# Hybrid decoder trunk: a planner that makes two plans, one with stretched times, redraws parts of each, and picks one by trial executions

## The chip, the cores and the metric

The kernel runs on one core of a Trainium2 chip, in one launch. The metric is the device time of one execution in microseconds (us), over several executions; lower is better. All times here are of this one core. PE is TensorE's matmul path, PEld its weight loads, DVE is VectorE, ACT is ScalarE, POOL is GpSimd and SP is SyncE, which issues most of the transfers.

## The reference

Two layers of a decoder on 1024 tokens of width 1024, in float32. Cut to what matters:

```python
def reference(x, attn_norm, w_in, ..., w_o, ffn_norm, w_gate_up, w_down, final_norm):
    for l in range(DEPTH):                         # 2
        h = rmsnorm(x, attn_norm[l])
        proj = h @ w_in[l]
        (c_q, c_kv, k_r, g_b, g_c, u_conv, u_pool, q_sw, k_sw, v_sw) = jnp.split(proj, pts, axis=-1)
        y_a = mla_attention(...)                   # 4 heads, causal over all keys
        y_b = short_gated_conv(...)                # causal, width 3
        y_c = multiscale_pool(...)                 # causal means over 2, 4, 8, 16
        y_d = swa_sink_attention(...)              # 4 heads, window of 128
        groups = jnp.stack([y_a, y_b, y_c, y_d], axis=2)
        gf = groups * lax.rsqrt(jnp.mean(groups * groups, axis=-1, keepdims=True) + RMS_EPS)
        x = x + (gf.reshape(b, s, D_MIX) * mix_norm[l]) @ w_o[l]
        h2 = rmsnorm(x, ffn_norm[l])
        gate, up = jnp.split(h2 @ w_gate_up[l], 2, axis=-1)
        x = x + (jax.nn.silu(gate) * up) @ w_down[l]     # D_FF = 2816
    return rmsnorm(x, final_norm)
```

## The kernel before

**The work.** Activations lie transposed, 128 channels on the partitions by 512 tokens, so a tile is 128 x 512 and the tokens make two halves. Each float32 operand is split into two fp32r parts, a rounded one and the rest, and `mm3` (L316) makes each product with three matmuls of up to 512 columns (recorded at L322). `split` (L340) makes the two parts: ACT copies the rounded one (L342), DVE subtracts it (L345). This is done for weights as they arrive and for activations as they are made. The two FFN products are done by a scheme with seven in place of eight block products: POOL and DVE form sums and differences of blocks (weights in `GateUp.sums`, L1260 to L1262; activations in `combine`, L1179 to L1200, and in `combos`, L1511 to L1516, which also stores them to HBM as `ad`), and the down projection loads `ad` again. The gate's step for an FFN block begins in `gu_start`; its L1380 takes a product out of PSUM on DVE. L421 is the common elementwise product on DVE, L1228 adds the output projection to the residual, L1309 and L1318 take first FFN products out of PSUM, L1500 and L1502 are the SiLU on ACT and the multiplication after it on POOL.

**Buffers.** Nearly all tiles live in 47 slots of 128 x 1024 (`u0` to `u46`, class `Slots`), and products in eight PSUM banks. Which slot a tile takes is decided as the program is written out: in turn, or, where planned times are given (`ends`), the slot whose last tile is planned to end first. The banks likewise: by fixed turns, or as a list (`given`).

**The order.** The program is first written out straight, and then ordered by a planner, class `Order` (L1858). It reads the written instructions and their dependencies, gives each a time on its engine (`costs`, L1934; for a DVE `TensorTensor` of n columns 0.15 + n x 0.001045 us, for a load its bytes' time + 2.1 us), and `run` (L1984) executes them on five queues, PE, ACT, DVE, POOL and SP: whenever an engine is free it takes the instruction of lowest rank among those that are ready. A load is taken to land 1.5 us late (`LATE`). While a DVE instruction with two inputs in SBUF and a POOL sum overlap, the later one is made to wait. `find` (L2055) goes forward with the written order as rank, back from the end to get a rank by urgency, and forward again, three forward runs in all, and keeps the shortest. `banks` (L2070) and `ends` (L2082) draw banks and slots from the planned times; they need a new writing-out, and so a new plan. `scheduled_kernel` (L2102) does this round four times, keeps the round with the shortest plan, and imposes its order on each queue (`impose`, L2089: each instruction is put behind the one before it, without a semaphore).

So every engine works its queue off strictly in the planned order. If the first in a queue waits on the chip longer than was planned, all behind it wait too.

Of the kernel before, what the change touches and what calls it, by code (L numbers as in the profile page):

```python
# [35 lines left out]
HALVES = (1, 0)  # L36
OUT_PARTS = tuple((d, t) for d in range(NK) for t in HALVES)
N_U = 47

NSP = 3  # L40
NG = NFF // 2
# [12 lines left out]
class Slots:  # L54
# [3 lines left out]
    def __init__(self, pool, n, ends=None):  # L58
        self.pool = pool
        self.ends = iter(ends) if ends else None  # L60
        self.until = [0.0] * n
        self.asked = []
        self.places = deque(range(n))
        self.halves = {F32: deque(), F32R: deque()}
        self.cur = [None] * n
        self.dt = [None] * n
# [56 lines left out]
def trunk_kernel(ctx: ExitStack, tc: tile.TileContext, ins, out, given=None, ends=None):  # L123
# [9 lines left out]

    slots = Slots(ctx.enter_context(tc.tile_pool(name="slots", bufs=1)), N_U, ends)
    R, F = View(slots, F32R), View(slots, F32)
# [1722 lines left out]
class Order:  # L1858
# [7 lines left out]
    SHARED = 1.3  # L1866
    LEAST = 0.14

    def __init__(self, traced, edges, banks=True):
        self.n = len(traced)  # L1870
        self.engine = [self.queue(i) for i in traced]
        self.cost = [self.costs(i) for i in traced]
        self.kind = [self.kinds(i) for i in traced]
        self.moved = [self.passing(i) for i in traced]
        place = {i.name: k for k, i in enumerate(traced)}
        need = [{} for _ in traced]
        users = self.users = defaultdict(list)
        for k, i in enumerate(traced):
            for m in {a.memref for a in (*i.outs, *i.ins) if hasattr(a, "memref")}:
                users[m].append(k)  # L1880
        freed = [set() for _ in traced]
        for k, i in enumerate(traced):
            for name, kind in edges(i.name):
                if name in place:
                    p = place[name]
                    need[k][p] = need[k].get(p, False) or "NoSync" not in str(kind)
                elif banks or self.engine[k] != "PE":
                    freed[k].update(place[x] for x, _ in edges(name) if x in place)
            for p in freed[k]:
                need[k][p] = True  # L1890
        for m, ks in users.items():
            made = [freed[k] for k in ks if any(m == getattr(a, "memref", 0) for a in traced[k].outs)]
            for p in set().union(*made).difference(ks):
                for k in ks:
                    if p < ks[0]:
                        need[k][p] = True
        self.need = [list(d.items()) for d in need]
        self.feeds = [[] for _ in traced]
        for k, d in enumerate(self.need):
            for p, sync in d:  # L1900
                self.feeds[p].append((k, sync))
# [79 lines left out]
            return 0.29 + n * 0.00098, 0.21 + n * 0.00098  # L1981
        return t, t - 0.083

    def run(self, rank, back=False):  # L1984

        ahead, wait = (self.need, self.feeds) if back else (self.feeds, self.need)
        late, cost, kind = self.LATE[back], self.cost, self.kind  # L1990
        left = [len(w) for w in wait]
        ready, end, free = [0.0] * self.n, [0.0] * self.n, dict.fromkeys(self.ENGINES, 0.0)
        later = {e: [] for e in self.ENGINES}
        now = {e: [] for e in self.ENGINES}
        order = {e: [] for e in self.ENGINES}
        flying, served = deque(), 0.0
        port = {"two": 0.0, "pool": 0.0}
        other = {"two": "pool", "pool": "two"}
        for k in range(self.n):
            if not left[k]:  # L2000
                heapq.heappush(later[self.engine[k]], (0.0, k))

        def due(e, t):
            while later[e] and later[e][0][0] <= t:
                k = heapq.heappop(later[e])[1]
                heapq.heappush(now[e], (rank[k], k))

        for _ in range(self.n):
            best = None
            for e in self.ENGINES:  # L2010
                due(e, free[e])
                if not now[e] and not later[e]:
                    continue
                t = free[e] if now[e] else later[e][0][0]
                if e == "SP" and not back and len(flying) == self.LANES:
                    t = max(t, flying[0])
                if best is None or t < best[0]:
                    best = t, e
            t, e = best
            due(e, t)  # L2020
            k = heapq.heappop(now[e])[1]
            seen, taken = cost[k]
            order[e].append(k)
            if back:
                free[e] = t + taken * (self.SHARED if kind[k] == "pool" else 1.0)
                end[k] = -free[e]
            else:
                if kind[k] in port:
                    more = max(0.0, port[other[kind[k]]] - t - self.LEAST)
                    seen, taken = seen + more, taken + more  # L2030
                    port[kind[k]] = t + seen
                free[e], end[k] = t + taken, t + seen
                if self.moved[k]:
                    if kind[k] == "load":
                        end[k] += late
                    served = end[k] = max(end[k], served + self.moved[k])
                if e == "SP":
                    flying.append(end[k])
                    if len(flying) > self.LANES:
                        flying.popleft()  # L2040
            for j, sync in ahead[k]:
                if back:
                    s, o = cost[j]
                    if kind[j] == "load":
                        s += late
                    r = free[e] + (self.HOP[self.engine[j]] + s - o if sync else -o)
                else:
                    r = end[k] + self.HOP[e] if sync else t
                ready[j] = max(ready[j], r)
                left[j] -= 1  # L2050
                if not left[j]:
                    heapq.heappush(later[self.engine[j]], (ready[j], j))
        return end, order

    def find(self, passes=3):  # L2055
        rank, best = list(range(self.n)), None
        for _ in range(passes):
            end, order = self.run(rank)
            if best is None or max(end) < best[0]:
                best = max(end), order, end  # L2060
            rank, _ = self.run([-x for x in end], back=True)
        return best

    def tiles(self, prefix):


        found = (m for m in self.users if m.startswith(prefix) and m.rsplit("_", 1)[1].isdigit())
        return sorted(found, key=lambda m: int(m.rsplit("_", 1)[1]))
# [30 lines left out]
                )  # L2099


def scheduled_kernel(fresh, ins_of, rounds=4):  # L2102

    def trace(banks, ends, order=None):
        nc = fresh()
        ins, out = ins_of(nc)
        with tile.TileContext(nc) as tc:
            asked = trunk_kernel(tc, ins, out, banks, ends)  # L2110
            traced = [
                i
                for i in nc.cur_bb.bb.instructions
                if Order.queue(i) in Order.ENGINES and i.opcode != "TilePoolBoundary"
            ]
            if order is not None:
                Order.impose(tc, traced, order)
        return nc, traced, asked

    nc, traced, asked = trace(None, None)  # L2120
    plan = Order(traced, nc.dependency_edges)
    end, best = plan.find()[2], None
    for _ in range(rounds):
        given = plan.banks(end), plan.ends(end, asked)
        nc, traced, asked = trace(*given)
        plan = Order(traced, nc.dependency_edges)
        span, order, end = plan.find()
        if best is None or span < best[0]:
            best = span, given, order
    return trace(*best[1], best[2])[0]  # L2130


# [131 lines left out]
```

## Time and profile before

| | |
|---|---|
| time, median of 3 runs | 2047.57 us (2047.41 to 2049.72) |
| profiled execution | 2048.33 us, span 2046.5 us |
| PE busy | 2029.3 us, 9422 matmuls |
| DVE busy | 1518.8 us, 2443 instructions |
| ACT busy | 989.4 us, 1737 instructions |
| POOL busy | 541.2 us, 412 instructions |
| DMA over the span | 305.50 MB, 149 GB/s on the mean |

The profile is of one execution. The span goes from the first to the last instruction's end; the execution's own time has 1.8 us around it. Busy time is the union of an engine's instructions; the matmuls overlap in the pipeline, and their ends are modelled. The view of waits says for each engine how long it stood idle in front of which line, and which line's instruction ended that. The timeline gives start, length, engine, line, output and input, with the idle time before in brackets. In the windows view each row is a stretch of the span with the busy time and instruction count of each engine. The chain is followed back from the last instruction, at each step to what released it.

### The profile page before, as it was taken

The numbers are of one execution on the slowest core, as the hardware profiler recorded it, in microseconds if no ns is written. First come the engines' busy times: TensorE is split into PE (matmuls) and PEld (weight loads), VectorE is DVE, ScalarE is ACT, GpSimd is POOL, SyncE is SP. The second block draws the span as 40 slices with busy tenths as digits, with TensorE's granted clock in tenths as the row PEclk, the third lists the DMA queues.
The fourth block names the chain that finished last, engine by engine and source line by source line (L and its number), as shares of the span: only waits on it lengthen the run. The fifth ranks groups of instructions, "written<-read, shape, count | busy, mean of one in ns | idle before, by whom it ended". The sixth has DMA issues, their size and how long they took to land.

```text
span 2046.5 us, 26478 instructions
## 1 busy us (share of the span) xinstructions
PE 2029.3 (99%) x9422; PEld 1676.5 (82%) x9422; DVE 1518.8 (74%) x2443; ACT 989.4 (48%) x1737; POOL 541.2 (26%) x412
## 2 busy tenths in 40 slices
PE   9999999999999999999999999999999999999998
PEld 7887888878888888888888878888788888888887
DVE  8779978997666768546656898889966666676555
ACT  7447657753333335434533666667433333354342
POOL 0100000047786782010001000000577654410000
PEclk9999999999999999999999999999999999999999
DMA  5431232334645556997426413232455522287552
GB/s 207 104 66 42 77 102 84 136 134 157 204 168 190 180 172 253 287 279 223 157 71 139 107 52 110 70 114 106 150 190 169 184 106 93 86 289 265 179 187 86
DMA packets 141348, 305.50 MB, mean 149 GB/s; under 512 B 13728, under 2 KB 56736, under 8 KB 141216
## 3 DMA queue, kind: packets, MB, share of 16 engines
q1 hardware_dynamic: 130976, 280.74, 39.9%
q0 software_dynamic: 10240, 23.07, 5.8%
q8 instruction: 74, 1.21, 0.2%
q14 instruction: 58, 0.48, 0.1%
HBM read 225.11 MB, written 100.66 MB: 159 GB/s over the span
## 4 chain that ended last, share of the span: by engine, by line
PE 93%; DVE 3%; ACT 1%; issue 1%; DMA 1%; POOL 0%; DVEq 0%; ACTq 0%; POOLq 0%
PE ps_mm L322 36%; PE ps_s L322 29%; PE ps_t L322 11%; PE ps_pv L322 8%; PE ps_pv L1090 2%; PE ps_t L1078 1%; DVE u L345 1%; PE ps_s L1024 1%; PE ps_s L1026 1%; PE ps_s L1025 1%; DMA u<-in_w_gu 1%; PE ps_s L896 1%; PE ps_pv L699 1%; PE ps_s L638 1%; PE ps_t L405 1%
## 5 line engine op out<-in xcount | busy, mean ns | idle before, releaser
L322 PE MATMUL ps_mm<-u,u 128*128 128x512 f32 (+1 forms) x3378 | 831.0, 390 | 2.9 <-DVE tp L1380 1.3
L322 PEld LDWEIGHTS ps_mm<-u,u 128*128 128x128 f32 x3378 | 615.3, 188 | 128.7 <-issue 5.5
L322 PE MATMUL ps_s<-u,u 128*128 128x512 f32 x2670 | 634.4, 390 | 2.3 <-DVE u L345 1.7
L345 DVE TENSOR_TENSOR u<-u,u 128x1024 fp32r<-128x1024 f32 (+2 forms) x400 | 449.5, 1142 | 213.1 <-ACT u L342 154.8
L322 PEld LDWEIGHTS ps_s<-u,u 128*128 128x128 f32 x2670 | 500.4, 188 | 110.1 <-DVE u L345 4.0
L342 ACT CAST u<-u 128x1024 fp32r<-128x1024 f32 (+2 forms) x400 | 346.4, 882 | 452.8 <-DMA u<-ad 75.8
L322 PE MATMUL ps_t<-u,u 128*128 128x512 f32 (+1 forms) x1124 | 254.4, 378 | 0.4 <-DVE u L1309 0.4
L322 PEld LDWEIGHTS ps_t<-u,u 128*128 128x128 f32 x1124 | 202.0, 188 | 41.4 <-DVE u L1494 2.0
L1502 POOL TENSOR_TENSOR tp<-tp,u 128x512 f32<-128x512 f32 x80 | 129.6, 1620 | 362.2 <-ACT tp L1500 362.1
L322 PE MATMUL ps_pv<-u,u 128*128 128x512 f32 x744 | 177.1, 389 | 0.0
L322 PEld LDWEIGHTS ps_pv<-u,u 128*128 128x128 f32 x744 | 139.6, 188 | 29.1
L1500 ACT ACTIVATE tp<-tp 128x512 f32<-128x512 f32 x80 | 50.6, 632 | 151.2 <-DVE tp L421 151.1
L1087 POOL MEMSET u<- 128x128 f32 x32 | 6.1, 221 | 406.6 <-PE ps_pv L1090 134.1
L342 ACT CAST u<-ps_t 128x512 fp32r<-128x512 f32 (+3 forms) x132 | 65.0, 503 | 47.6 <-PE ps_t L1078 23.3
L345 DVE TENSOR_TENSOR u<-ps_t,u 128x512 fp32r<-128x512 f32 (+3 forms) x132 | 75.3, 581 | 11.7 <-ACT u L342 9.7
L348 DVE SCALAR_TENSOR_TENSOR u<-u,par,u 128x512 fp32r<-128x512 f32 x100 | 73.3, 745 | 13.1 <-ACT u L347 12.8
L347 ACT ACTIVATE u<-u,par 128x512 fp32r<-128x512 f32 x100 | 70.2, 716 | 26.6 <-DVE u L421 10.6
L386 ACT ACTIVATE tn<-u 128x512 f32<-128x512 f32 (+1 forms) x91 | 52.9, 596 | 55.5 <-DVE u L1771 46.8
L296 POOL DMA_DIRECT2D gd<-in_w_gu x24 | 21.3, 887 | 217.8 <-DMA gd<-in_w_gu 57.6
L1290 POOL TENSOR_TENSOR u<-u 128x512 f32<-128x512 f32 x38 | 67.5, 1776 | 40.0 <-DVE u L345 38.8
L421 DVE TENSOR_TENSOR tp<-tp,u 128x512 f32<-128x512 f32 x76 | 68.7, 904 | 1.7
L1580 POOL TENSOR_TENSOR u<-u,u 128x352 f32<-128x352 f32 x48 | 62.9, 1311 | 3.1 <-DMA u<-in_w_dn 2.0
(206 smaller groups left out, 2356.4 us busy)
## 6 DMA issues: line engine op xcount, KB each, us to landing
u<-in_w_gu SPq DMA_DIRECT2D x84, 512.0 KB, 4.1
ad<-u SPq DMA_DIRECT2D x154, 256.0 KB, 2.4
u<-ad SPq DMA_DIRECT2D x70, 512.0 KB, 5.5
u<-in_w_dn SPq DMA_DIRECT2D x48, 352.0 KB, 3.5
qd<-u SPq DMA_DIRECT2D x48, 352.0 KB, 2.6
u<-qd SPq DMA_DIRECT2D x32, 512.0 KB, 5.4
u<-in_w_in SPq DMA_DIRECT2D x28, 512.0 KB, 3.5
u<-in_w_dn SPq DMA_DIRECT2D x24, 512.0 KB, 5.4
```

Source lines behind the costliest of these rows:

```text
L322: last_mm = pe.matmul(o, w, r, start=start and k == 0 and i == 0, stop=stop and k == n - 1 and i == 2, skip_group_check=again,)
L342: a = act.copy(hi, f)
L345: dve.tensor_tensor(out=lo, in0=f, in1=rd(hi), op=ALU.subtract)
L347: a = act.activation(hi, f, AF.Copy, scale=gain)
L348: dve.scalar_tensor_tensor(out=lo, in0=f, scalar=gain, in1=rd(hi), op0=ALU.mult, op1=ALU.subtract)
L386: act.activation(q, f, AF.Square)
L421: dve.tensor_tensor(out=o, in0=a, in1=b, op=ALU.mult)
L1090: pe.matmul(py[:, c0:], v_of(j, h), R.ap(s)[:, c0:], start=j == 0 and n == 0, stop=j == nj - 1 and n == 1,)
L1290: pool.tensor_tensor(out=q4, in0=q4, in1=F.ap(self.raw[1] + 1), op=ALU.add)
L1500: last_silu = act.activation(g, g, AF.Silu)
L1502: pool.tensor_tensor(out=g, in0=g, in1=r, op=ALU.mult)
L1580: pool.tensor_tensor(out=o, in0=a, in1=b, op=ALU.add)
```

## The change

The instructions themselves stay as they are: no part of `trunk_kernel` is touched. What is new is how the planner finds the order, the slots and the banks.

- The rounds go from four to one, for each of two plans. The first plans with the times of `costs`, the second with the times of DVE and ACT instructions multiplied by 1.03 (`SLOW`). Each starts from the straight program's plan with the same factor.
- `improve` takes a plan and its rank and draws 30 times: it picks a planned wait of PE of over 0.05 us, with a chance by its length, adds Gaussian noise with a deviation of 1 us to the rank of every instruction that is planned to end between 40 us ahead of that wait and 5 us behind it, plans anew with it, and keeps the new rank where the plan is not longer.
- `trial` executes a finished order six times in the model, the queues in fixed order and with the unchanged times, where in each execution a DMA load is late with a chance of a quarter, by up to 2.5 us, and the times of DVE, ACT and POOL vary by 2%. The plan with the shorter mean is taken.

```diff
+SLOW = (1.0, 1.03)
...
-    def run(self, rank, back=False):
+    def run(self, rank, back=False, fixed=None, draw=None):
...
+        if fixed is None:
+            cost = [
+                (a * self.slow, b * self.slow) if e in ("DVE", "Activation") else (a, b)
+                for (a, b), e in zip(cost, self.engine)
+            ]
...
+                if fixed is not None:
+                    i = len(order[e])
+                    if i == len(fixed[e]) or left[fixed[e][i]]:
+                        continue
+                    t = max(free[e], ready[fixed[e][i]])
...
+            if draw:
+                late = 2.5 * draw.random() if draw.random() < 0.25 else 0.0
+                if e in ("DVE", "Activation", "Pool"):
+                    more = draw.gauss(0.0, 0.02) * seen
+                    seen, taken = seen + more, taken + more
...
+    def trial(self, order):
+        ends = (self.run(None, fixed=order, draw=random.Random(n))[0] for n in range(6))
+        return sum(map(max, ends)) / 6
...
+    def waits(self, order, end):
+        found, free = [], 0.0
+        for k in order["PE"]:
+            seen, taken = self.cost[k]
+            start = end[k] - seen
+            if start - free > 0.05:
+                found.append((start, start - free))
+            free = start + taken
+        return found
+
+    def improve(self, best, tries):
+        draw = random.Random(1)
+        span, order, end = best
+        rank, _ = self.run([-x for x in end], back=True)
+        e, o = self.run(rank)
+        if max(e) <= span:
+            span, order, end = max(e), o, e
+        found = self.waits(order, end)
+        for _ in range(tries):
+            at = draw.choices([t for t, _ in found], [w for _, w in found])[0]
+            new = [
+                r + draw.gauss(0.0, 1) if at - 40 < t < at + 5 else r for r, t in zip(rank, end)
+            ]
+            e, o = self.run(new)
+            if max(e) <= span:
+                rank, span, order, end = new, max(e), o, e
+                found = self.waits(order, end)
+        return span, order, end
...
-def scheduled_kernel(fresh, ins_of, rounds=4):
+def scheduled_kernel(fresh, ins_of, rounds=1):
...
-    plan = Order(traced, nc.dependency_edges)
-    end, best = plan.find()[2], None
-    for _ in range(rounds):
-        given = plan.banks(end), plan.ends(end, asked)
-        nc, traced, asked = trace(*given)
-        plan = Order(traced, nc.dependency_edges)
-        span, order, end = plan.find()
-        if best is None or span < best[0]:
-            best = span, given, order
+    first, tried, found = Order(traced, nc.dependency_edges), asked, []
+    for slow in SLOW:
+        plan, asked, first.slow = first, tried, slow
+        end = plan.find()[2]
+        for _ in range(rounds):
+            given = plan.banks(end), plan.ends(end, asked)
+            nc, traced, asked = trace(*given)
+            plan = Order(traced, nc.dependency_edges, slow)
+            best = plan.find()
+            end = best[2]
+            order = plan.improve(best, 30)[1]
+            found.append((plan.trial(order), given, order))
+    best = min(found, key=lambda x: x[0])
     return trace(*best[1], best[2])[0]
```

More of the change, by code (lines that the diff above doesn't have):

```diff
@@ L2 @@
 import math
+import random
 from collections import defaultdict, deque
@@ L1867, with __init__ @@
     LEAST = 0.14
-    def __init__(self, traced, edges, banks=True):
+    def __init__(self, traced, edges, slow=1.0, banks=True):
+        self.slow = slow
         self.n = len(traced)
@@ L2010, in run @@
             for e in self.ENGINES:
[L2011 to L2014, printed above, removed]
+                if fixed is not None:
[3 more added lines that the diff above has]
+                    t = max(free[e], ready[fixed[e][i]])
+                else:
+                    due(e, free[e])
+                    if not now[e] and not later[e]:
+                        continue
+                    t = free[e] if now[e] else later[e][0][0]
                 if e == "SP" and not back and len(flying) == self.LANES:
@@ L2019, in run @@
             t, e = best
-            due(e, t)
-            k = heapq.heappop(now[e])[1]
-            seen, taken = cost[k]
+            if fixed is not None:
+                k = fixed[e][len(order[e])]
+            else:
+                due(e, t)
+                k = heapq.heappop(now[e])[1]
+            seen, taken = cost[k]
+            if draw:
[3 more added lines that the diff above has]
+                    seen, taken = seen + more, taken + more
             order[e].append(k)
@@ L2050, in run @@
                 left[j] -= 1
-                if not left[j]:
+                if not left[j] and fixed is None:
                     heapq.heappush(later[self.engine[j]], (ready[j], j))
         return end, order
+    def trial(self, order):
+        ends = (self.run(None, fixed=order, draw=random.Random(n))[0] for n in range(6))
+        return sum(map(max, ends)) / 6
     def find(self, passes=3):
```

## The prediction

> **What bounds the kernel now.** I read the page first, its busy shares and its chain of what ended last.
>
> ```profile
> span 2046.5 us, 26478 instructions
> PE 2029.3 (99%) x9422; PEld 1676.5 (82%) x9422; DVE 1518.8 (74%) x2443; ACT 989.4 (48%) x1737; POOL 541.2 (26%) x412
> ...
> PE 93%; DVE 3%; ACT 1%; issue 1%; DMA 1%; POOL 0%; DVEq 0%; ACTq 0%; POOLq 0%
> ```
>
> TensorE (PE) is busy for 2029.3 of 2046.5 us and carries 93% of the chain; DVE, the next engine, is at 74%. So the work of PE sets the time, and the change can only move the 17.2 us in which PE is idle. How fast PE goes while it is busy comes from the groups by form and from the chain in order of time.
>
> ```profile
> L322 PE MATMUL ps_s<-u,u 128*128 128x512 f32 x2670 | 634.4, 390 | 2.3 <-DVE u L345 1.7 <-DVE u L1228 0.4 <-ACT u L1318 0.2
> ...
> 446.98 2.72 PE ps_pv L322 x12
> ```
>
> Twelve matmuls of 512 columns take 2.72 us on the chain, 0.227 us each, while a single one shows 0.390 us from start to end. So PE must be held up by 0.390 - 0.227 = 0.163 us before any idle time shows at all: a wait costs the idle time that is shown plus up to 0.16 us. Next, the two ends of the program (the timeline).
>
> ```profile
> 1.06 5.49 PE L541 MATMUL ps_pv<-ones 128*128 128x128 f32 x24 [1.06 <-DVE ones L145]
> ...
> 2036.73 0.70 PE L409 MATMUL ps_s<-tn,ones 128*128 128x256 f32 x2 [0.59 <-ACT tn L408]
> ```
>
> PE starts 1.06 us after the span does, and its last matmuls end at 2036.73 + 0.70 = 2037.43, which leaves 2046.5 - 2037.4 = 9.1 us for the last normalisation and stores. With the 0.59 us before those matmuls that makes 10.7 us with no other matmul to stand in, and I take it that no order of the rest shortens them. What is left is 17.2 - 10.7 = 6.5 us. The view of the waits of PE gives nearly all of it:
>
> ```profile
> PE ps_s L322 <- DVE u L345: 1.7, 3, 1.1
> PE ps_mm L322 <- DVE tp L1380: 1.3, 1, 1.3
> PE ps_pv L541 <- DVE ones L145: 1.1, 1, 1.1
> PE ps_mm L322 <- ACT u L342: 0.7, 1, 0.7
> PE ps_s L409 <- ACT tn L408: 0.6, 1, 0.6
> PE ps_mm L322 <- DVE u L345: 0.5, 1, 0.5
> PE ps_s L1026 <- DVE u L345: 0.5, 1, 0.5
> PE ps_s L322 <- DVE u L1228: 0.4, 1, 0.4
> PE ps_t L322 <- DVE u L1309: 0.4, 1, 0.4
> PE ps_s L638 <- DVE u L345: 0.2, 1, 0.2
> PE ps_s L322 <- ACT u L1318: 0.2, 1, 0.2
> PE ps_mm L322 <- DVE te L421: 0.2, 1, 0.2
> ```
>
> Without L541 and L409, the two ends, ten rows remain: 12 waits, 6.1 us. With 0.163 us for each the most that a better order can win is 6.1 + 12 x 0.163 = 8.1 us. Where they lie, from the windows around the entries to the FFN (after the length: PE, PEld, DVE, ACT and POOL busy, each with its count):
>
> ```profile
> 408.00:446.00 38.00, 36.52 (x159) 29.11 (x158) 35.29 (x48) 21.30 (x35) 13.19 (x8) 1.00 0.29 96
> ...
> 1377.00:1445.00 68.00, 65.60 (x282) 52.25 (x281) 66.04 (x100) 49.80 (x81) 5.59 (x4) 1.00 0.31 108
> ```
>
> In layer 0's entry PE is idle for 38.00 - 36.52 = 1.5 us; these are two of the three waits of the first row. In layer 1's it is 68.00 - 65.60 = 2.4 us, in six waits: on ACT L342, DVE L345 (0.5, and the last 0.2 of the first row), L1228, L1309 and ACT L1318. DVE is busy there for 35.29 of 38.00 and 66.04 of 68.00 us: it is all but full, and PE waits for the operands that DVE splits. The largest wait outside is the 1.3 us on L1380; the other three, 0.5 + 0.2 + 0.2, lie in attention. Here is what stands behind the 1.3 us, from the chain in order of time:
>
> ```profile
> 1673.35 2.28 DMA ad<-u
> ...
> 1675.72 1.06 ACT u L342
> ...
> 1677.94 0.70 DVE tp L1380
> ```
>
> A store of a slot lands 2.28 us after its issue, the cast of L342 has waited for it, the subtraction of L345 waits for the cast, and behind that one on DVE's queue stands L1380, which needs nothing of it; PE waits for L1380. It is the order of DVE's queue, and a slot that a store still held, that make PE pay.
>
> **The change, part by part.** The work is the same: the functions that emit instructions are not touched, so 9422 matmuls stay and cost 0. What moves is the order on each of the five queues, SP's and POOL's among them, and the slots and banks.
>
> First, **the shake**. It draws new ranks for whatever the plan ends between 40 us ahead of a planned wait of PE and 5 us behind, 30 times for each plan, and keeps what doesn't lengthen the plan. It can only find waits that the plan foresees, so the question is how true the plan's durations are.
>
> ```profile
> 1671.24 1.22 DVE L345 TENSOR_TENSOR u<-u,u 128x1024 fp32r<-128x1024 f32 x1
> ```
>
> The program's own cost function gives 0.15 + 1024 x 0.001045 = 1.22 us for this subtraction of 1024 columns, as in the row of the timeline. So waits on a full DVE are in the plan and can be shaken, as ten of the twelve are by the engine they wait for. What is one order worth against another? Both layers do the same work at the FFN entry, and the two orders differ by 2.4 - 1.5 = 0.9 us and four waits, 0.9 + 4 x 0.163 = 1.6 us. I take it that 30 draws bring layer 1's entry at least to layer 0's: -1.6 us. Bounds: 0, if a full DVE leaves no better order, and all of both entries, 3.9 + 8 x 0.163 = 5.2 us. Below 0 it can't go in the plan's own terms, since a longer plan is dropped.
>
> Second, **the late transfer**. The 1.3 us depend on slots and queue positions that are all drawn anew; layer 0 has no such wait at the same place, so it goes: 1.3 + 0.16 = -1.5 us. Bounds: the whole 1.5 gained, or one more of its kind, +1.5. The attention's 0.9 us I leave as they are (bounds: 0.9 + 3 x 0.163 = 1.4 either way).
>
> Third, **one round where there were four**, and **3% on DVE's and ACT's times** in the second plan. Before, the slots and banks came out of up to four rounds, the shortest plan of them kept; now each plan has one. The trace doesn't show what a round is worth. The two layers of this trace are the nearest thing, two orders for one kind of work: 1.5 + 0.4 = 1.9 us of waits in layer 0, 2.4 + 1.3 + 0.5 = 4.2 in layer 1. So I bound it by 2.3 us, either way, and take 0, since the shake that follows draws from the same scatter. The 3% only space the plan further than the durations above ask for; they add no instruction, and with a second candidate they can be refused: 0.
>
> Fourth, **the trials**. The page's row of the loads from ad:
>
> ```profile
> u<-ad SPq DMA_DIRECT2D x70, 512.0 KB, 5.5
> ```
>
> A load of 512 KB is 1.31 + 2.1 = 3.4 us in the cost functions, to which planning adds 1.5 (4.9), the trials on average 0.25 x 1.25 = 0.3 (3.7). The row has 5.5. So the trials, which also stir the times of DVE, ACT and POOL by 2%, see too little of late loads; I give the choice nothing, 0, between the 2.3 us of two orders either way.
>
> Sum: -1.6 - 1.5 = -3.1 us. The profiled execution took 2048.33 us, 1.83 more than its span and 0.76 more than the median of the three runs, 2047.57. It would become 2045.2; the median 2044.5.
>
> **The rivals.** *Most waits go.* If the draws clear both FFN entries and the transfer, 5.2 + 1.5 = 6.7 us are gained: 2040.9. For it: the plan's durations are true, and no wait but one is over 1.1 us. Against: DVE's 66.04 of 68.00.
>
> *The order is as good as it gets*, or the change doesn't do what it says because 30 draws from one round only come back to where four rounds were: within 1 us of now, 2047.5. For it: PE at 99%.
>
> *More slots come behind transfers*, and it gets slower. With one round the slots follow a single planning pass whose buffers still lay in turn, and the trials hardly see late loads. ACT's waits for loads show how much is exposed:
>
> ```profile
> ACT u L342 <- DMA u<-ad: 75.8, 44, 6.2
> ```
>
> In 44 waits ACT stood still, up to 6.2 us, and nearly all of it stayed hidden from PE. Each that comes through costs what the one at 1677 us costs, 1.5 us. Against the forecast's gain it takes two to be back at no change, and (3.1 + 4.1) / 1.46, five of the 44, to be slower by over 0.2% (4.1 us, about what a measurement of this kernel can tell from no change). With six: 2044.5 + 8.8 = 2053.3.
>
> *POOL and DVE collide.* The rows of the timeline just behind the wait on L1380:
>
> ```profile
> 1667.26 0.69 DVE L421 TENSOR_TENSOR tp<-tp,u 128x512 f32<-128x512 f32 x1
> ...
> 1678.54 1.99 DVE L345 TENSOR_TENSOR u<-u,u 128x1024 fp32r<-128x1024 f32 x1
> 1679.40 2.28 POOL L1260 TENSOR_TENSOR u<-u,u 128x512 f32<-128x512 f32 x1
> 1680.45 1.77 DVE L421 TENSOR_TENSOR tp<-tp,u 128x512 f32<-128x512 f32 x1
> ```
>
> While POOL's sums run, the subtraction takes 1.99 in place of 1.22 us and the product of L421 1.77 in place of 0.69, 0.77 and 1.08 more, and POOL is drawn out too. An order that puts POOL's additions into the full stretches of DVE hands this on to PE; at 0.92 on the mean it takes (3.1 + 4.1) / 0.92, eight new collisions there, to be slower by over 0.2%: 2044.5 + 7.4 = 2051.9. The Trainium skill ("SBUF — State Buffer", "Who interferes with whom") speaks against any reordering in these words: "Issue order, not op shape, decides who blocks." The trace agrees as far as 1.99 against 1.22 us goes. Against this rival: the planner counts such an overlap, in planning and in the trials.
>
> **How the numbers follow.** The forecast, 2044.5 with a range of its own from 2043 to 2046: 0.34, a third of it below 2043.5. Most waits go: 0.24. As good as it gets: 0.17. Slots behind transfers: 0.18, of which 0.02 stay within 0.2%. Collisions: 0.07. Faster by over 0.2%: 0.24 + 0.11 = 0.35. Slower: 0.16 + 0.07 = 0.23. Within 0.2%: 0.42. The range starts at 2040.0, just above 2047.6 - 8.1 = 2039.5 where no wait would be left, and goes to 2053.5, with six transfers come through.
>
> **What would show it.** PE's busy time stays at 2029 us within 1 us, with 9422 matmuls; otherwise the first step is wrong. If the forecast holds, PE's waits without the two ends sum to some 4 us in 7 or 8 groups, layer 1's entry is at 1.5 us or less, and none of the waits on a store or load reaches 1 us. More than 8 us of waits, of which most end with a DMA two steps up the chain, would be the transfers; long DVE rows beside POOL's inside 358 to 460 or 1381 to 1443 us the collisions. If PE's idle time falls but the time doesn't, the view of waits was the wrong measure.

## The result: 0.9964 of the time before, and the profile after

| | before | after |
|---|---|---|
| median, us | 2049.15 (2047.41 to 2049.72, 6 runs) | 2041.41 (2040.91 to 2042.12, 6 runs) |
| ratio | | 0.9964, 95% interval 0.9951 to 0.9977 |
| profiled execution, us (span) | 2048.33 (2046.5) | 2041.27 (2039.5) |

The kernel became faster by 0.36%, 7.4 us by that ratio (the two medians differ by 7.7); the profiled executions differ by 7.1. A second measurement of the same program, among the experiments, gave 0.9969. Lines of the code after stand two further down than before (L345 is L347, L1380 is L1382).

The page of the kernel after, its busy shares and its chain:

```profile
span 2039.5 us, 26480 instructions
PE 2024.4 (99%) x9422; PEld 1676.1 (82%) x9422; DVE 1528.1 (75%) x2443; ACT 990.1 (49%) x1737; POOL 540.6 (27%) x412
...
PE 94%; DVE 3%; ACT 1%; DMA 1%; issue 0%; POOL 0%; SPq 0%; DVEq 0%; ACTq 0%
```

PE's idle time is 2039.5 - 2024.4 = 15.1 us, only 2.1 less than before. The other 4.9 us came out of what the page calls busy, with the same 9422 matmuls. The view of the waits of PE, after:

```profile
PE ps_mm L324 <- DVE u L219: 1.1, 2, 1.0
PE ps_pv L543 <- DVE ones L147: 1.1, 1, 1.1
PE ps_mm L324 <- ACT u L349: 0.7, 3, 0.3
PE ps_s L411 <- ACT tn L410: 0.6, 1, 0.6
PE ps_mm L324 <- DVE u L350: 0.6, 2, 0.3
PE ps_s L324 <- DVE u L347: 0.6, 1, 0.6
PE ps_t L324 <- DVE u L1496: 0.4, 1, 0.4
PE ps_t L324 <- DVE u L1230: 0.3, 1, 0.3
PE ps_s L324 <- ACT u L1320: 0.3, 1, 0.3
PE ps_t L407 <- DVE u L718: 0.3, 1, 0.3
```

The 1.3 us on L1380 are gone; a new one of 1.0 us on L219, a weight split, has come. Without the two ends there are 4.3 us where there were 6.1. That is not 7 us. The windows around the FFN's entries show more, in the first count, the number of matmuls that PE got done:

```profile
408.00:446.00 38.00, 37.44 (x165) 30.56 (x164) 35.25 (x46) 21.10 (x34) 16.84 (x9) 1.00 0.33 112
1377.00:1445.00 68.00, 67.70 (x299) 55.65 (x298) 65.04 (x99) 48.73 (x80) 9.24 (x6) 1.00 0.29 106
```

In the same 38 us there were 159 matmuls before and are 165 now; in the same 68 us 282 before and 299 now. At the pace of 0.227 us the entries have given 6 x 0.227 = 1.4 and 17 x 0.227 = 3.9 us, 5.3 of the 7.0 that the spans differ by. Their idle time went from 1.5 to 0.6 and from 2.4 to 0.3 us, by 3.0. (In these two windows the counts repeat within one matmul, 0.23 us, in a second profile of either program.) So a wait costs more than it shows. Of the other 1.7 us, some 1.1 lie around the old wait on L1380, where PE got 88 matmuls done in place of 83 (86 in the second profile); the kernel before first:

```profile
1664.00:1684.00 20.00, 18.70 (x83) 15.16 (x82) 14.01 (x15) 6.53 (x9) 7.37 (x6) 1.00 0.37 132
1664.00:1684.00 20.00, 19.88 (x88) 16.14 (x87) 17.20 (x18) 9.00 (x12) 9.86 (x7) 1.00 0.33 119
```

The rest, the new wait on L219, the warm-up told of at the end and small waits in attention, was not split further. Two neighbours in the timeline of the kernel before let one see where the hidden part of a wait lies:

```profile
1436.03 1.02 PE L322 MATMUL ps_mm<-u,u 128*128 128x512 f32 x3 [0.74 <-ACT u L342]
1437.55 2.33 PE L322 MATMUL ps_mm<-u,u 128*128 128x512 f32 x9 [0.49 <-DVE u L345]
```

From 1436.03 to 1437.55 PE began three matmuls, 0.68 us of work at its pace. 0.84 us were lost, and the row shows 0.49 of idle. Of the 0.35 us that don't show, 0.16 are the overlap that the prediction counts, and 0.18 lie inside the first row: its three matmuls take 1.02 us, where 2 x 0.227 + 0.390 = 0.84 would do.

### The profile page after: what moved, and what is told of

It reads as the page before. It is cut to its first block, busy times and chain, and to the rows that moved or that the text cites. A ratio compares the mean times of both kernels' runs of the same rounds, so it can differ in the third digit from the quotient of the medians.

```text
span 2039.5 us, 26480 instructions
## 1 busy us (share of the span) xinstructions
PE 2024.4 (99%) x9422; PEld 1676.1 (82%) x9422; DVE 1528.1 (75%) x2443; ACT 990.1 (49%) x1737; POOL 540.6 (27%) x412
## 4 chain that ended last, share of the span: by engine, by line
PE 94%; DVE 3%; ACT 1%; DMA 1%; issue 0%; POOL 0%; SPq 0%; DVEq 0%; ACTq 0%
PE ps_mm L324 36%; PE ps_s L324 30%; PE ps_t L324 11%; PE ps_pv L324 8%; PE ps_pv L1092 2%; PE ps_t L1080 1%; DVE u L347 1%; PE ps_s L1026 1%; PE ps_s L1028 1%; PE ps_s L1027 1%; PE ps_s L640 1%; PE ps_pv L701 1%; PE ps_t L407 1%; PE ps_t L689 1%; PE ps_s L898 0%; DVE u L423 0%
## 5 line engine op out<-in xcount | busy, mean ns | idle before, releaser
L347 DVE TENSOR_TENSOR u<-u,u 128x1024 fp32r<-128x1024 f32 (+2 forms) x400 | 457.3, 1162 | 196.0 <-ACT u L344 144.6
L347 DVE TENSOR_TENSOR u<-ps_t,u 128x512 fp32r<-128x512 f32 (+3 forms) x132 | 75.2, 581 | 14.9 <-ACT u L344 13.8
L388 ACT ACTIVATE tn<-u 128x512 f32<-128x512 f32 (+1 forms) x91 | 52.5, 595 | 50.3 <-DVE u L1773 48.1
L1370 ACT COPY tn<-ps_s 128x512 f32<-128x512 f32 x61 | 35.8, 587 | 64.3 <-PE ps_s L324 64.0
```

Source lines behind the costliest of these rows:

```text
L347: dve.tensor_tensor(out=lo, in0=f, in1=rd(hi), op=ALU.subtract)
L388: act.activation(q, f, AF.Square)
L1370: act.copy(o, p)
```

## The experiments

The theory from the two traces was that the **stretch** makes the gain: with DVE's and ACT's times put 3% too long, results are planned to be ready a little before PE needs them, and on the chip small delays no longer reach PE. The rivals: the **shake** clears the waits, as I had predicted; or it is **scatter**, any other order moving the time by some us. The window counts are from 408 to 446 us and from 1377 to 1445 us.

| run | stretch | draws | median, us | ratio to before | 95% interval | matmuls in the windows |
|---|---|---|---|---|---|---|
| before | 0 | 0 | | 1 | | 159, 282 |
| e1_first_round | 0 | 0, one round | 2049.00 | 1.0004 | 0.9995 to 1.0013 | 159, 282 |
| e2_shake_only | 0 | 30 | 2051.18 | 1.0015 | 1.0005 to 1.0024 | 156, 284 |
| f4_plain_other_draws | 0 | 30, other seed | 2051.32 | 1.0014 | 1.0005 to 1.0023 | 155, 280 |
| f1_plain_150 | 0 | 150 | 2050.86 | 1.0014 | 1.0005 to 1.0024 | 160, 285 |
| e3_stretch_only | 3% | 0 | 2045.50 | 0.9985 | 0.9975 to 0.9995 | 165, 293 |
| e4_both (the kernel after) | 3% | 30 | 2042.04 | 0.9969 | 0.9958 to 0.9981 | 166, 298 |
| f2_both_other_draws | 3% | 30, other seed | 2042.88 | 0.9974 | 0.9964 to 0.9984 | 166, 299 |
| f3_both_150 | 3% | 150 | 2043.21 | 0.9975 | 0.9965 to 0.9985 | 166, 299 |
| g1_both_1015 | 1.5% | 30 | 2045.45 | 0.9983 | 0.9974 to 0.9992 | 159, 287 |
| g2_true_stt | 0, one cost raised | 30 | 2046.87 | 0.9993 | 0.9983 to 1.0003 | 166, 291 |
| g3_true_stt_stretch | 3%, one cost raised | 30 | 2045.79 | 0.9984 | 0.9975 to 0.9993 | 161, 290 |
| h1_trials_true | 0, 3, 3.5% | 3 x 30 each | 2042.56 | 0.9969 | 0.9957 to 0.9981 | 160, 295 |

### Four rounds or one

The kernel before, with

```diff
-def scheduled_kernel(fresh, ins_of, rounds=4):
+def scheduled_kernel(fresh, ins_of, rounds=1):
```

> The kernel before with one round in place of four, nothing else. The planner of the kernel before turns out to have kept its first round, so every queue's order comes out as it was. All theories: ratio 1.000 to the kernel before, within 0.1%. If it is not, the spread between executions of one program is larger than thought, and no smaller difference can be read.

Measured 1.0004, the interval holds 1, and both windows count the same matmuls. The rounds that were dropped had given nothing. The run also shows how well the window counts repeat.

### One part at a time

Each is the kernel after with edits to two lines: the stretches that are planned, and whether the draws are made. "Draws" stands for all of `improve`, which begins with one more pass back and forward.

```diff
 e2_shake_only
-SLOW = (1.0, 1.03)
+SLOW = (1.0,)
 e3_stretch_only
-SLOW = (1.0, 1.03)
+SLOW = (1.03,)
-            order = plan.improve(best, 30)[1]
+            order = best[1]
```

e4_both is the kernel after, unchanged.

> The changed kernel with the first plan alone (times not stretched), shaken by 30 draws. Theory 'shake' (my prediction's step: the draws clear the waits at the full stretches of DVE): 0.9965, some 7 us under the kernel before, with layer 1's entry to the FFN at 0.5 us of idle PE in place of 2.4. Theory 'stretch' (the gain is the slack that 3% longer times of DVE and ACT leave between a result and its use): 0.999 to 1.000, with the waits at both entries as before. Theory 'scatter' (any other order moves the time by some us either way): anything from 0.996 to 1.003.

> The changed kernel with the stretched plan alone and no draws. Theory 'stretch': 0.997, nearly all of the gain, layer 1's entry under 1 us of idle PE. Theory 'shake': 1.000 to 1.002, with waits of over 2 us at layer 1's entry. Theory 'scatter': anything from 0.996 to 1.003, and not near the kernel after.

> The changed kernel itself once more, beside the others. All theories: 0.9965, 7 us under the kernel before. It is the stretched, shaken plan that the trials chose, so e3 and e4 differ by the 30 draws alone: theory 'stretch' expects them within 1.5 us of each other, theory 'shake' some 7 us apart.

The shake alone made the kernel slower, 1.0015. The stretch alone gave 0.9985, 3.0 us, less than half of the gain; with the draws on top it is 0.9969. The executions of e3 and e4 don't overlap (2044.3 to 2046.57 and 2040.59 to 2043.01), so the draws do help once the plan is stretched, by 3.5 us, more than half of the gain. "Shake" is refuted as the cause; "stretch" is too small by itself; and from three points "scatter" could not be ruled out. Where the stretch alone gains and what it leaves open, in its windows:

```profile
408.00:446.00 38.00, 37.46 (x165) 30.55 (x164) 34.64 (x45) 22.64 (x36) 15.55 (x8) 1.00 0.30 93
1377.00:1445.00 68.00, 66.71 (x293) 54.36 (x292) 65.97 (x99) 49.12 (x81) 7.86 (x4) 1.00 0.32 113
```

Layer 0's entry is as good as in the kernel after (165), layer 1's goes from 282 to 293 of the 299. The shake alone, same view:

```profile
408.00:446.00 38.00, 36.60 (x156) 28.70 (x155) 34.16 (x45) 23.67 (x37) 10.87 (x7) 1.00 0.22 77
1377.00:1445.00 68.00, 65.84 (x284) 52.75 (x284) 66.02 (x100) 47.35 (x77) 5.54 (x3) 1.00 0.29 102
```

156 and 284: neither entry moved.

### Scatter, or what the plan says

Four more orders, by other draws and more of them.

```diff
 f1_plain_150 and f4_plain_other_draws:  SLOW = (1.0,)
 f2_both_other_draws and f3_both_150:    SLOW = (1.03,)
 f1 and f3:
-            order = plan.improve(best, 30)[1]
+            order = plan.improve(best, 150)[1]
 f2 and f4:
-        draw = random.Random(1)
+        draw = random.Random(3)
```

> The first plan alone (times not stretched), with 150 draws in place of 30. By the planner's own count this is the shortest plan of all, shorter than that of the kernel before and than that of the kernel after, and its trials come out shorter than those of the kernel after as well. Theory 'plan' (time on the chip follows the plan's length with the unstretched times, so enough draws do it without a stretch): 0.996 to 0.997, at or below the kernel after. Theory 'slack' (the stretch is what makes a plan hold on the chip): 0.999 to 1.001, as e2. Theory 'scatter': anything from 0.996 to 1.003.

> The stretched plan, shaken by 30 draws from another seed. Its plan and its trials are as short as those of the kernel after. Theory 'plan' and theory 'slack': 0.997, within 1.5 us of the kernel after. Theory 'scatter' (the kernel after was a lucky order): anything from 0.996 to 1.003, as likely beside the stretched plan without draws (0.9985) as beside the kernel after.

> The stretched plan with 150 draws. The draws shorten the stretched plan further, but with unstretched times its trials come out longer than those of the kernel after and like those of the stretched plan without draws. So it tells apart which count the chip follows. Theory 'slack' (the stretched length counts): 0.996 to 0.9965, below the kernel after. Theory 'plan' (the unstretched trials count): 0.9985, as e3. Theory 'scatter': anything from 0.996 to 1.003.

> The first plan alone (not stretched), 30 draws from another seed, which shorten its plan where those of e2 did next to nothing; in the trials it is no better than the kernel before. Theory 'plan' by planned length: 0.999; by the trials: 1.000 to 1.001. Theory 'slack': 1.000 to 1.0015, as e2. Theory 'scatter': anything from 0.996 to 1.003.

Three unstretched, shaken orders: 1.0015, 1.0014, 1.0014. Three stretched, shaken ones: 0.9969, 0.9974, 0.9975. All six intervals leave out 1, on the two sides of it, and no interval of one group touches one of the other. So which draws are taken is not the cause: inside a group they differ by 0.06% at most. But `scheduled_kernel` draws slots and banks before `improve`, once for each stretch. The orders of a group share them, and the six runs compare two plans, not six. Whether the 3% gain by the order or by the slots and banks that came with it was not separated. Other plans do scatter more: those below with longer durations give 0.9969 to 0.9993. That all of them lie under the 1.0014 of the unstretched plan with draws speaks for longer durations as the cause; the size of the gain depends on the plan.

The plan's own count is no guide either. By its expectation f1 had the shortest plan and trials shorter than those of the kernel after, and it was slower than the kernel before by 0.14%. f3 should have been below the kernel after by its stretched length, or like e3 by its trials; it lies between, and its interval reaches both. f1's page:

```profile
PE 2031.2 (99%) x9422; PEld 1675.2 (82%) x9422; DVE 1514.9 (74%) x2443; ACT 990.1 (48%) x1737; POOL 540.2 (26%) x412
...
PE 90%; DVE 5%; DMA 2%; ACT 2%; issue 1%; POOL 1%; SPq 0%; DVEq 0%; ACTq 0%; POOLq 0%
```

Against the page after: PE is held busy for 6.8 us more with the same matmuls (1 us of it the warm-up told of at the end), and the chain runs over DVE for 5% in place of 3%, over DMA for 2% in place of 1% and over PE for 90% in place of 94%. One reading is that the draws tightened the order until what PE needs came just in time by the plan's durations, and on the chip it came late. It is not shown: by f4's expectation the draws of e2 did next to nothing to the length of its plan, and e2 is as slow as f1. Nor do single profiles place the loss: in the first 60 us f1 got 249 matmuls done and the kernel before 261, but e1_first_round, with the order of the kernel before, got 254. f1's waits, the first of 15 rows and the next two beside the ends:

```profile
PE ps_mm L324 <- DVE tp L1382: 1.2, 2, 1.0
...
PE ps_s L640 <- DVE u L621: 0.9, 1, 0.9
PE ps_s L324 <- DVE u L1230: 0.9, 1, 0.9
```

### How much stretch, and what it makes up for

```diff
 g1_both_1015:         SLOW = (1.015,)
 g2_true_stt:          SLOW = (1.0,)
 g3_true_stt_stretch:  SLOW = (1.03,)
 g2 and g3, in the costs of DVE:
-            t = 0.15 + n * 0.00109
+            t = 0.187 + n * 0.00109
```

> The changed kernel with one plan, DVE's and ACT's times stretched by 1.5% in place of 3%, 30 draws. Theory 'slack in proportion': half the stretch, half the gain: 0.999, and some 290 matmuls in the window from 1377 to 1445 us. Theory 'true times' (the stretch only makes up for DVE's times being put too short, by 1 to 2% on the mean, so 1.5% is enough): 0.997, and 298 matmuls there. Theory 'threshold above 1.5%': 1.000 to 1.0015, 280 to 285 matmuls, as in the three unstretched plans with draws.

> No stretch. Only the cost of one kind of DVE instruction is put right: the one with a scalar operand (L348 of the kernel before) is planned with 0.15 + 512 x 0.00109 = 0.708 us and takes 0.745 us in the profile's row, so its fixed part becomes 0.187. 30 draws, one plan. Theory 'true times': 0.997 to 0.998, the gain of the stretch without one, 165 matmuls in the window 408 to 446 us. Theory 'slack' (margin on every DVE and ACT time is needed, for what differs from execution to execution and for what the plan leaves out): 1.000 to 1.0015, 155 to 160 matmuls there.

> That cost put right and the 3% stretch on top, 30 draws, one plan. If both matter it is below the kernel after, 0.996; if 3% was already enough, 0.997, as the three stretched and shaken plans; if more margin costs more than it saves, 0.998 to 0.999.

With draws, 0, 1.5 and 3% gave 1.0014 to 1.0015, 0.9983 and 0.9969 to 0.9975. g1 is nearest to "in proportion", by the clock (0.999 lies in its interval) and by the second window (287, expected some 290); the 0.997 and 298 matmuls of "true times" lie outside. Raising the one cost brought 1.0015 to 0.9993 (e2 and g2, with the same seed), and 156 and 284 matmuls to 166 and 291. Two rows of the kernel before, the one on which that edit rests and one that speaks against it:

```profile
L348 DVE SCALAR_TENSOR_TENSOR u<-u,par,u 128x512 fp32r<-128x512 f32 x100 | 73.3, 745 | 13.1 <-ACT u L347 12.8
L417 DVE SCALAR_TENSOR_TENSOR u<-tn 128x512 f32<-128x512 f32 x33 | 22.6, 685 | 0.4
```

100 of the first take 745 ns and were planned with 708. But the edited line of `costs` holds for every `scalar_tensor_tensor` on DVE, not only for those with a scalar operand from SBUF. The 33 of L417 take 685 ns, and groups of L388, L414 and L1494 take 684 to 686; for these 708 was long enough, and 745 is a margin of 9%. So g2 is a correction in one part and a stretch in another, and it doesn't tell the two apart. What it shows is that longer times for one kind of DVE instruction, with none for ACT, move both entries. It is not the whole gain, since 0.9993 stays above 0.9974 and its interval holds 1. What else comes late was not separated: the transfers, that POOL and DVE hold each other up, or delays of single instructions. More margin on top was no better (g3, 0.9984).

The counts at the two entries do not rank whole plans: g2 has 166 and 291 with 0.9993, and h1 below has 160 and 295 with 0.9969.

### A choice with truer trials

```diff
-SLOW = (1.0, 1.03)
+SLOW = (1.0, 1.03, 1.035)
+LONG = 1.015
...
+                if e in ("DVE", "Activation"):
+                    seen, taken = LONG * seen, LONG * taken
...
-    def improve(self, best, tries):
+    def improve(self, best, tries, seed):
-        draw = random.Random(1)
+        draw = random.Random(seed)
...
-            order = plan.improve(best, 30)[1]
-            found.append((plan.trial(order), given, order))
+            for seed in (1, 2, 3):
+                order = plan.improve(best, 30, seed)[1]
+                found.append((plan.trial(order), given, order))
```

> A version that uses what the runs before showed: stretches of 0, 3 and 3.5%, three shakes of 30 draws each, and trials in which DVE's and ACT's times are 1.5% longer than in the cost functions. With such trials the nine plans run so far fall into the order that the chip gave: unstretched last, 1.5% and 3% without draws between, 3% with draws first. Theory 'margin' (the trials' choice holds on the chip once their times are true): 0.9955 to 0.9965, below the kernel after. Rival 'scatter' (below 0.1% the choice means nothing): 0.997 to 0.998, as the other two stretched and shaken plans.

0.9969, as e4; no version beat the kernel after. The interval reaches into the ranges of both theories, so the run doesn't decide between "margin" and "scatter" among stretched plans. What such trials do keep out, by what the expectation says of the nine plans, are the unstretched ones.

## Why the prediction was right, and where its steps were not

The direction was right and the time lies in the range, in good part by luck: the range went from 2040.0 to 2053.5, a gain of over 0.2% had a chance of 0.35, and of the two steps that made up the forecast one, the shake, made the kernel slower by itself. The forecast, 2044.5, was 3 us too high; the time was that of the rival "most waits go" (2040.9, chance 0.24). That rival had the right places, both entries of the FFN and the late transfer, and the wrong cause: the draws clear these waits only on the stretched plan.

**The work is the same: right, but the sign that was to show it was wrong.** There are 9422 matmuls as before, but PE's busy time fell by 4.9 us where I had said within 1; 1.1 of these are the warm-up. Busy time holds the short delays of PE too, since a matmul is drawn for 0.39 us and the next can start after 0.227.

**A wait costs what is shown and 0.16 us: too little.** At the two entries the waits went from 8 to 2 and the idle time by 3.0 us, while 5.3 us of matmuls were gained: (5.3 - 3.0) / 6 = 0.4 us beside what is shown for each. With 0.4 in place of 0.16 the bound of 8.1 us on all gain would be some 10.9 (6.1 + 12 x 0.4, an estimate), though no run came to either. "If PE's idle time falls but the time doesn't, the view of waits was the wrong measure" has a twin that I had not thought of: the span fell by 7.0 us and the idle time by 2.1.

**The shake, -1.6 us: this step failed.** On the unstretched plan it gave +0.14% to +0.15% in three runs and moved no entry by more than 4 matmuls; on the stretched plan the same draws gave 3.5 us (e4 against e3). I had checked the plan's durations on one row, the subtraction of L345, whose 1.22 us fit, and had concluded that the plan's waits were those of the chip. The row of L348 on the page, 745 ns against 708, was there to be read: 18 of these lie in layer 1's window, 18 x 0.037 = 0.7 us on a DVE that is full for 66 of 68 us. Why the draws lose on the unstretched plan stays open.

**The 3%, taken as 0: the term that was mis-sized.** I had written "The 3% only space the plan further than the durations above ask for" and given them nothing. They gave -0.15% alone and some -0.4% against the same draws without them, with the slots and banks that came with them. The upper bound that I gave for the shake at both entries, 5.2 us, is about what they gave (5.3 measured), but with the stretch under the draws.

**One round for four, 0: right for another reason.** I had argued that it scatters within 2.3 us; it is the same program.

**The late transfer, -1.5 us: right in the profile of the kernel after.** No row of L1382 is left there. In the second profile of the same program this wait is back with 0.5 us:

```profile
PE ps_mm L324 <- DVE tp L1382: 0.5, 1, 0.5
```

So it comes and goes from execution to execution, and where it comes it shows 0.5 us in place of 1.3.

**The trials, 0.** They chose the stretched plan, which was worth 9 us against the other one that they had (e4 against e2, 2042.04 and 2051.18). They saw the right thing, but barely: with 150 draws in place of 30 they would have preferred f1, by what its expectation says of its trials, and the change would have been slower.

**POOL and DVE collide.** They do, but it is not shown that they do so more often than before. L421 took 904 ns on the mean and takes 955, L345 1142 and now 1162, and DVE is busy for 1528.1 us in place of 1518.8. With its order unchanged, e1_first_round has 923 ns, 1156 ns and 1522.9 us, and the second profile of the kernel after 933 ns, 1161 ns and 1525.0 us. L421 of the kernel before and of e1_first_round:

```profile
L421 DVE TENSOR_TENSOR tp<-tp,u 128x512 f32<-128x512 f32 x76 | 68.7, 904 | 1.7
L421 DVE TENSOR_TENSOR tp<-tp,u 128x512 f32<-128x512 f32 x76 | 70.2, 923 | 1.7
```

The kernel after:

```profile
L423 DVE TENSOR_TENSOR tp<-tp,u 128x512 f32<-128x512 f32 x76 | 72.6, 955 | 1.9
...
L347 DVE TENSOR_TENSOR u<-u,u 128x1024 fp32r<-128x1024 f32 (+2 forms) x400 | 457.3, 1162 | 196.0 <-ACT u L344 144.6
```

In the full stretch from 1377 to 1445 us DVE's busy time is 65.04 us now and was 66.04, so nothing was added there. The Trainium skill ("SBUF — State Buffer", "Who interferes with whom") has the rule that the issue order decides who blocks. No run here tells the effect of another order from the scatter of one order, and it set no part of the result.

**More slots behind transfers**: not seen; no wait of PE in the kernel after is over 1.0 us inside the program.

## What to carry to other kernels

This static order was better planned with durations a few per cent too long on the engines that feed the bottleneck: the same random search gave a slower kernel with unstretched durations, with three sets of draws, and a faster one with a 3% margin, with three. Check the planner's durations against every large group of the profile, not against one, and a cost formula against every group that it covers. And to size a change at one place, count the bottleneck's instructions in a window of fixed length rather than adding up its idle time: the counts showed 5.3 us where the idle time showed 3.0.

## What the runs showed of the hardware that I had not expected

The 24 warm-up matmuls at the start can take a different time in two executions of one program: the timeline's first rows, of the kernel after and of e4_both.

```profile
1.06 4.42 PE L543 MATMUL ps_pv<-ones 128*128 128x128 f32 x24 [1.06 <-DVE ones L147]
5.75 0.50 PE L324 MATMUL ps_mm<-u,u 128*128 128x512 f32 x1 [0.28 <-ACT u L349]
6.54 0.73 PE L324 MATMUL ps_mm<-u,u 128*128 128x512 f32 x2 [0.29 <-DVE u L350]
```

```profile
1.06 5.22 PE L543 MATMUL ps_pv<-ones 128*128 128x128 f32 x24 [1.06 <-DVE ones L147]
```

In the kernel before it was 5.49 us. It is worth little, since PE waits for its first operands right after, 0.28 and 0.29 us in the rows shown. So up to 1.1 us of the fall in PE's busy time between the two pages need not be an effect of the change: two executions of one program differ by 0.8. In both kernels the median of the 24 is 0.421 us, but the shortest takes 0.421 before and 0.274 after, at a granted clock of 1.00 in the windows of both. The Trainium skill ("TensorE: Matmul & The Clock Gate", "What's actually happening") says that TensorE's clock is held back until a window of activity has passed, and that this window runs freely, so that where it falls varies. The shorter matmuls would fit that, but the granted clock of these rows doesn't show the change.
